# The low half of the gated rows by an accumulating DMA from GpSimd instead of a VectorE subtraction

## The chip, the cores and the metric

The kernel runs as one program on one core of one Trainium2 chip. The metric is the device time of one execution in microseconds (us), as the median of several executions; lower is better. The kernel before has a median of 2209.8 us over three runs (2206.93 to 2212.24). TensorE (PE) does the matrix products, VectorE (DVE) and ScalarE (ACT) the elementwise work, GpSimd (POOL) small copies and sums, and SyncE (SP) issues most of the loads and stores.

## The reference, cut to what matters

The program is one layer of a streaming encoder for 2048 prompt tokens and 64 sample tokens, with a model width of 1024. The first half (normalisation, input projection, pooling mixer, mLSTM memory, output projection) is not touched. The second half is a gated MLP with a causal convolution of width 3 between its two projections:

```
h2   = rmsnorm(x, g2) * (1 + sc2) + sh2
up   = h2 @ w_up                                   # 1024 -> 2 * 2816
conv = b_conv + sum(w_conv[j] * upp[:, j:j + T] for j in range(3))
a, g = jnp.split(conv, 2, -1)
x    = x + gt2 * ((jax.nn.silu(g) * a) @ w_down)   # 2816 -> 1024
```

All inputs and outputs are float32. The product silu(g) * a, channel by channel, is what this text calls the gated rows. They are the moving operand of the product with w_down.

## The kernel before, in words

**Halves.** TensorE takes operands that are rounded to a shorter float32 form (fp32r). So every operand X of a large product is kept as a high half (X rounded to that form, made by a copy on ScalarE) and a low half (X minus the high half, made by a subtraction on VectorE). A product is three passes: high by high, high weight by low row, low weight by high row. They stand in this order in the tuple PASSES.

**Tiling.** Tokens are handled transposed: channels on the 128 partitions, tokens along the row. The 2112 tokens of the MLP are three groups of 704, and a group is two halves of 352, the width of one matmul. The last group holds the end of the prompt and the 64 sample tokens, with separate pieces for each, so that an operation there is often two or three instructions. The 2816 inner channels are 22 tiles f of 128. Each group goes through them in four parts (PARTS) of 5, 5, 6 and 6 tiles. There are thus twelve parts in all, and 66 pairs (group, f), where a pair is one tile of a and the matching tile of g.

**The up phase of a part.** For each f, an object Pair makes a and g by seven products of 12 matmuls each (`Pair.products`, line 1522 records the matmuls), which share work between the two token halves by sums of weights and of rows. Between the products it issues steps of the pair before (old) and of the one before that (older). The steps of one pair, in their order, are:

- copy_u4, sum_g1, sum_a, sum_g0: the last sums out of the banks into the extended rows ea and eg (VectorE, line 1530). GpSimd first fills the two columns ahead of the row (line 1488).
- scale_a, scale_g: ta and tg, the convolution's first term, by ScalarE (line 1505). GpSimd then saves the row's last two columns (lines 1499 to 1502).
- taps_a, taps_g: the other two terms, two VectorE instructions each (line 1510).
- silu: on tg in place, ScalarE (line 1616).
- gate: tg = ta * tg, VectorE (line 1620).
- split_hi: the high half of the gated row, a ScalarE copy from tg to av (line 1637).
- split_lo: the low half, a VectorE subtraction of the high half from tg into the other half of av (line 1645).

The tile tg comes from a pool with one buffer (`t = f1.tile([P, EX], F32, tag="t" + tag, ...)`, the pool f1 having bufs=1). So scale_g of the next pair writes the bytes that split_hi and split_lo of this pair read. The tile av has six buffers, one for each pair of a part.

**The down phase of a part.** `down(ps, W, ks, secs)` multiplies the part's av tiles by tiles of w_down (line 1785): six matmuls of 352 columns for each k, three passes by two token halves. After each k it issues one of the steps that wait in the list `todo`. The order for a part with nf tiles is: n = 0 over k = 0 to nf-3; the remaining steps; the twelve matmuls of the last pair's last product; n = 1 over k = 0 to nf-3; k = nf-2 for n = 0 and 1; n = 2 over k = 0 to nf-2; k = nf-1 for n = 0, 1, 2; then the rows n = 3 to 7 in full. The next-to-last pair's split stands in `todo` under n = 0, and the last pair's steps from sum_g0 to split_lo stand under n = 1 and after. So av of the last two pairs is made while TensorE is already multiplying the earlier ones.

**What sets the order.** In this stage TensorE, ScalarE, VectorE and GpSimd run in the order of the program text (tc.manual_schedule). Each engine works its own list from the front and waits, at an instruction, for what that needs. SyncE's loads of weights run ahead of use through `pump`, which also issues the weights' own split into halves (ScalarE line 366, VectorE line 369). GpSimd has no DMA of its own before: every transfer is issued from SyncE or ScalarE.

Of the kernel before, what the change touches and what calls it, by code (L numbers as in the profile page):

```python
# [9 lines left out]
F32 = mybir.dt.float32  # L10
F32R = mybir.dt.float32r
AF = mybir.ActivationFunctionType
ALU = mybir.AluOpType
# [46 lines left out]
def tile_layer(ctx: ExitStack, tc: tile.TileContext, xT, vecs, cst, rst, rowv, w_mod, w_ada, w_qkou, w_v, w_pool,  # L60
               w_out, w_up, w_down, st_C, st_pool, yT, o_pool, o_C, o_m, o_conv):
    nc = tc.nc
    act, dve, pool, pe = nc.scalar, nc.vector, nc.gpsimd, nc.tensor
# [16 lines left out]
    def mm_ps():  # L80
        return bank("mm")
# [18 lines left out]
    def tick(i=0):  # L100
        q = bg[i]
        while q:
            try:
                next(q[0])
                return
            except StopIteration:
                q.pop(0)
# [54 lines left out]
    def pair_of(t, row, n):  # L162

        return t[:, :2 * row].rearrange("p (a t) -> p a t", a=2)[:, :, :n]
# [1310 lines left out]
    todo = []  # L1475

    def do(n=1):

        for _ in range(n):
            if todo:  # L1480
                todo.pop(0)()

    def both_of(a, b):
        return lambda: (a(), b())

    def ext_tile(o, f, tag):
        ext = f1.tile([P, EX], F32, tag="e" + tag, name="e" + tag, bufs=EB)
        pool.tensor_copy(ext[:, 0:2], UC[:, f, :])
        if o.last:
            pool.tensor_copy(ext[:, PT + 2:PT + 4], V[:, V_SC + 2 * f:V_SC + 2 * f + 2])  # L1490
        return ext
# [21 lines left out]
    def spans(o, half):  # L1513

        return [(pa, pb, a + 2 + 2 * s) for (i, pa, pb, a, b, s) in o.pieces if i == half]

    def product(ps, Bo, nm, first):
        pump()
        U = get_unit()
        for kc in range(4):  # L1520
            for pi, (a, b) in enumerate(PASSES):
                pe.matmul(ps[:, :FH], U[:, a, kc * P:(kc + 1) * P], Bo.at(nm, kc, b),  # L1522
                          start=(first and kc == 0 and pi == 0), stop=(kc == 3 and pi == 2), skip_group_check=not first)
            if kc % 2:
                tick(0)
        live[0] -= 1
# [5 lines left out]
    def half_tile(nm):  # L1532
        return f1.tile([P, FH], F32, tag=nm, name=nm)

    class Pair:
# [9 lines left out]
        def products(self, old):  # L1545


            o, Bo, f = self.o, self.Bo, self.f
            self.before = old
            older = old and old.before  # L1550
            b1, b2 = self.b1, self.b4 = mm_ps(), mm_ps()

            def rest(*steps):
                for pair, step in steps:
                    if pair:
                        step(pair)
            rest((old, Pair.copy_u4), (older, Pair.gate))
            product(b1, Bo, "B11", True)
            rest((old, Pair.sum_g1), (old, Pair.sum_a))
            self.s1 = half_tile("s1")  # L1560
            act.activation(self.s1, b1[:, :FH], AF.Copy)
            rest((older, Pair.split_hi))
            product(b2, Bo, "B21", True)
            rest((old, Pair.scale_a), (older, Pair.split_lo))
            if old:
                old.last_product()
            rest((old, Pair.taps_a), (old, Pair.sum_g0))
            product(b1, Bo, "T2", False)
            self.u2 = half_tile("u2")
            act.activation(self.u2, b1[:, :FH], AF.Copy)  # L1570
            rest((old, Pair.scale_g))
            self.ea = ext_tile(o, f, "a")
            for (a, b, d) in spans(o, 0):
                dve.tensor_tensor(out=self.ea[:, d:d + b - a], in0=b2[:, a:b], in1=self.s1[:, a:b], op=ALU.add)  # L1574
            self.b3 = mm_ps()
            product(self.b3, Bo, "T3", True)
            rest((old, Pair.taps_g))
            tick(1)
            product(self.b4, Bo, "B22", True)
            rest((old, Pair.silu))  # L1580
            product(b1, Bo, "T1", False)
# [40 lines left out]
        def split_hi(self):  # L1622
            t = f2.tile([P, XT], F32R, tag="av", name="av", bufs=6)
            self.apart = not (self.o.last and self.f >= PARTS[-1][0])
            if self.apart:
                d = t.rearrange("p (a h t) -> p a h t", a=2, h=2)
                w = NUDGE if self.i == 1 else 0
                self.cuts = [(lambda b, i=i, pa=pa, pb=pb: d[:, b, i, pa + w * b * i:pb + w * b * i], a + 2 * s, b + 2 * s)
                             for (i, pa, pb, a, b, s) in self.o.pieces] if self.o.last or w else [
                    (lambda b: d[:, b, :, :FH], 0, FT)]  # L1630
                self.av[self.i] = lambda b, lo, hi: d[:, b, lo // FH, w * b * (lo // FH):w * b * (lo // FH) + hi - lo]
            else:
                d = pair_of(t, 2 * XR, FT)
                self.cuts = [(lambda b, lo=a, hi=e: d[:, b, lo:hi], a + 2 * s, e + 2 * s) for (a, e, s) in self.o.segs]
                self.av[self.i] = lambda b, lo, hi: d[:, b, lo:hi]
            for cut, a, b in self.cuts:
                act.activation(cut(0), self.of_tg(cut(0), a, b), AF.Copy)  # L1637

        def of_tg(self, like, a, b):
            v = self.tg[:, a:b]  # L1640
            return v.rearrange("p (h t) -> p h t", h=2) if len(like.shape) == 3 else v

        def split_lo(self):
            for cut, a, b in self.cuts:
                dve.tensor_tensor(out=cut(1), in0=self.of_tg(cut(0), a, b), in1=cut(0).bitcast(F32), op=ALU.subtract)  # L1645

    def reload(Bo):
        for nm in BN:
# [104 lines left out]
    for o in fgroups:  # L1753
        Bo = B[o.g]
        for pi, (f0, f1_) in enumerate(PARTS):
# [4 lines left out]
            pair = None  # L1760
            for f in range(f0, f1_):
                old, pair = pair, Pair(o, Bo, f, f - f0, av)
# [17 lines left out]
            def down(ps, W, ks, secs, stays=False):  # L1780
                for k in ks:
                    U = W.at(k // 4)
                    for (a, b) in PASSES:
                        for i, (lo, hi) in enumerate(secs):
                            pe.matmul(ps[i][:, :hi - lo], U[:, a, k % 4 * P:(k % 4 + 1) * P], av[k](b, lo, hi),  # L1785
                                      start=(k == 0 and (a, b) == PASSES[0]), stop=(k == nf - 1 and (a, b) == PASSES[-1]))
                    if (k % 4 == 3 or k == nf - 1) and not stays:
                        live[0] -= 1
                    pump()
                    if todo:  # L1790
                        do()
                    else:
                        tick(1 - k % 2)
# [23 lines left out]

            old = pair.before
            pair.copy_u4()
            todo.extend([both_of(pair.sum_g1, old.gate), both_of(pair.sum_a, old.split_hi), both_of(old.split_lo, pair.scale_a)])  # L1820
            for n in range(NE - 1):
                pss.append([mm_ps() for _ in both])
                down(pss[n], Ws[n], range(nf - 2), both)
                if n == 0:
                    do(9)
                    pair.last_product()
                    todo.extend([both_of(pair.sum_g0, pair.scale_g), pair.taps_a, pair.taps_g, pair.silu, pair.gate,
                                 pair.split_hi, pair.split_lo])
            for n in range(NE - 1):
                down(pss[n], Ws[n], [nf - 2], both)  # L1830
            pss.append([mm_ps() for _ in both])
# [102 lines left out]
```

## Time and profile before

| what | value |
|---|---|
| median of three runs | 2209.8 us (2206.93 to 2212.24) |
| span of the profiled execution, first to last instruction | 2205.6 us |
| the median beyond that span | 4.2 us |
| TensorE busy | 2186.1 us, 99% of the span |
| VectorE busy | 1568.5 us, 71% |
| ScalarE busy | 1005.3 us, 46% |
| GpSimd busy | 203.0 us, 9% |
| mean granted clock of TensorE | 0.999 |
| line 1645, the subtraction | 112 instructions, 62.0 us |
| line 1637, the high half | 112 instructions, 56.2 us |

The profiled execution's own time is given by its span alone; the runs' times hold some us of start and end beside it. The gated rows are made from 828 to 2157 us of the span. The subtraction is 36 instructions of 704 columns, 32 of 352, 16 of 288 and 22 of 64, and 6 of 640 that are left. A row of a group reads: line, engine, operation, out<-in, shapes, count | busy us, mean ns of one | idle time of the engine just before them and what ended it. A row of the timeline reads: start in us, duration, engine, line, operation, count, and in brackets the engine's idle time before it and its releaser. Adjacent like instructions are merged into one row.

### The profile page before, as it was taken

Reading aid. Unit: us, or ns where it says so; the run is one execution under the profiler, and the core shown is the slowest. Engines: PE = TensorE matmul, PEld = TensorE weight load, DVE = VectorE, ACT = ScalarE, POOL = GpSimd, SP = SyncE. Lnnn points to the kernel's source line nnn. Section 1 sums busy time; section 2 is a strip of 40 time slices with the busy share of each in tenths; the row PEclk is TensorE's granted clock in tenths of the full one; section 3 lists DMA queues with packets and bytes.
Section 4 is the critical chain, followed back from the end, with each engine's and each line's share of the span. In section 5 each row is a group of like instructions: output and inputs, shape, how many; then the busy total and the mean of one; then the engine's idle time right before and its main releaser. Section 6 shows DMA issues by size and latency. Waiting matters only on the chain. (4 is left out here: it accounts for less than half of the span.)

```text
span 2205.6 us, 38165 instructions
## 1 busy us (share of the span) xinstructions
PE 2186.1 (99%) x13804; PEld 2079.2 (94%) x13804; DVE 1568.5 (71%) x2916; ACT 1005.3 (46%) x1993; POOL 203.0 (9%) x481
## 2 busy tenths in 40 slices
PE   8999999999999999999999999999999999999998
PEld 7888888888899999999999999999999999999998
DVE  5887669577765778787958587767667685767474
ACT  4653334235243455554636354545344443445354
POOL 0010000001000100010000210000001210101012
PEclk9999999999999999999999999999999999999999
DMA  9977987997898695767557876565458565353442
GB/s 355 367 242 264 333 275 243 324 324 239 292 323 272 223 310 177 234 205 239 188 173 233 266 245 200 183 214 175 144 169 285 186 190 166 111 173 121 150 148 81
DMA packets 279357, 498.58 MB, mean 226 GB/s; under 512 B 25176, under 2 KB 105432, under 8 KB 279168
## 3 DMA queue, kind: packets, MB, share of 16 engines
q1 hardware_dynamic: 267392, 468.05, 65.0%
q10 hardware_dynamic: 11776, 28.09, 3.4%
q8 instruction: 109, 1.79, 0.3%
q14 instruction: 80, 0.66, 0.1%
HBM read 385.29 MB, written 110.75 MB: 225 GB/s over the span
## 5 line engine op out<-in xcount | busy, mean ns | idle before, releaser
L1522 PE MATMUL mm<-hx,wt 128*128 128x352 f32 x5544 | 885.4, 321 | 1.0 <-DVE ea L1574 0.9
L1522 PEld LDWEIGHTS mm<-hx,wt 128*128 128x128 f32 x5544 | 879.5, 188 | 2.1 <-ACT wt L366 1.5
L1785 PE MATMUL mm<-av,wt 128*128 128x352 f32 (+2 forms) x3168 | 508.6, 321 | 0.4 <-DVE av L1645 0.3
L1785 PEld LDWEIGHTS mm<-av,wt 128*128 128x128 f32 x3168 | 502.6, 188 | 3.0 <-DVE av L1645 0.9
L423 PE MATMUL mm<-hl,wt 128*128 128x512 f32 (+2 forms) x1920 | 395.8, 358 | 1.7 <-DMA wt<-hl_kept 1.7
L366 ACT ACTIVATE wt<-raw 128x512 fp32r<-128x512 f32 (+3 forms) x494 | 274.5, 571 | 249.6 <-PE mm L1785 109.3
L369 DVE TENSOR_TENSOR wt<-raw,wt 128x512 fp32r<-128x512 f32 (+3 forms) x494 | 307.0, 637 | 87.5 <-ACT wt L366 81.4
L423 PEld LDWEIGHTS mm<-hl,wt 128*128 128x128 f32 x1920 | 312.6, 188 | 49.4 <-issue 5.3
L1800 DVE SCALAR_TENSOR_TENSOR x<-mm,MOD,x 128x352 f32<-128x352 f32 (+4 forms) x224 | 106.5, 526 | 128.8 <-PE mm L1785 128.8
L423 PE MATMUL mm<-mx,wt 128*128 128x512 f32 (+1 forms) x960 | 186.8, 353 | 0.0
L423 PEld LDWEIGHTS mm<-mx,wt 128*128 128x128 f32 x960 | 158.8, 188 | 25.4 <-ACT mx L1378 1.1
L1510 DVE SCALAR_TENSOR_TENSOR tg<-eg,V,tg 128x704 f32<-128x704 f32 (+1 forms) x132 | 125.7, 952 | 49.3 <-ACT tg L1505 46.8
L369 DVE TENSOR_TENSOR wt<-wt 128x512 fp32r<-128x512 f32 x176 | 121.8, 692 | 49.4 <-ACT wt L366 49.2
L366 ACT ACTIVATE wt<-wt 128x512 fp32r<-128x512 f32 x176 | 110.2, 626 | 75.1 <-DMA wt<-wsum 62.5
L1510 DVE SCALAR_TENSOR_TENSOR ta<-ea,V,ta 128x704 f32<-128x704 f32 (+1 forms) x132 | 125.6, 952 | 7.8 <-ACT ta L1505 5.4
L1645 DVE TENSOR_TENSOR av<-tg,av 128x704 fp32r<-128x704 f32 (+4 forms) x112 | 62.0, 588 | 43.2 <-ACT av L1637 43.0
L1570 ACT ACTIVATE u<-mm 128x352 f32<-128x352 f32 x66 | 30.6, 464 | 120.3 <-PE mm L1522 81.8
L1616 ACT ACTIVATE tg<-tg 128x704 f32<-128x704 f32 (+1 forms) x66 | 52.3, 793 | 68.9 <-DVE tg L1510 68.9
L203 DVE SCALAR_TENSOR_TENSOR acc<-raw,CA,acc 128x512 f32<-128x512 f32 x84 | 60.5, 744 | 32.1 <-DMA raw<-w_ada 32.1
L1530 DVE TENSOR_TENSOR eg<-mm,u 128x352 f32<-128x352 f32 x154 | 70.1, 467 | 18.4 <-ACT u L1585 11.2
L1114 PE MATMUL mm<-wt,hl 128*128 128x256 f32 (+1 forms) x576 | 70.9, 282 | 0.0
L1114 PEld LDWEIGHTS mm<-wt,hl 128*128 128x128 f32 x576 | 69.3, 188 | 1.0 <-issue 0.6
(299 smaller groups left out, 1951.9 us busy)
## 6 DMA issues: line engine op xcount, KB each, us to landing
wt<-hl_kept SPq DMA_DIRECT2D x108, 512.0 KB, 5.9
raw<-w_up SPq DMA_DIRECT2D x198, 256.0 KB, 3.1
wt<-wsum SPq DMA_DIRECT2D x176, 256.0 KB, 4.0
wt<-wsplit SPq DMA_DIRECT2D x88, 512.0 KB, 3.9
raw<-w_down SPq DMA_DIRECT2D x96, 256.0 KB, 3.9
w<-w_up SPq DMA_DIRECT2D x88, 256.0 KB, 5.4
wsum<-w SPq DMA_DIRECT2D x44, 512.0 KB, 5.7
wsplit<-wt SPq DMA_DIRECT2D x44, 512.0 KB, 5.0
```

The source lines that it names most:

```text
L203: dve.scalar_tensor_tensor(out=acc[s], in0=w, scalar=CA[:, k, s:s + 1], in1=acc[s], op0=ALU.mult, op1=ALU.add)
L366: act.activation(u.w[:, 0, :u.n], u.raw[:, :u.n], AF.Copy)
L369: dve.tensor_tensor(out=u.w[:, 1, :u.n], in0=u.raw[:, :u.n], in1=u.w[:, 0, :u.n].bitcast(F32), op=ALU.subtract)
L423: pe.matmul(ps[bi][:, :hi - lo], U[:, a, k % 4 * P:(k % 4 + 1) * P], mv[k][:, b, lo:hi], start=(at == 0 and pi == 0), stop=(k == order[-1] ...
L1114: pe.matmul(ps[ti][:n, :cols], h[4 * kh + k4][:, b, lo:lo + n], U[:, a, k4 % 2 * cols:(k4 % 2 + 1) * cols], start=(kh == 0 and k4 == 0 and ...
L1510: dve.scalar_tensor_tensor(out=t[:, :E], in0=ext[:, j:j + E], scalar=wc(j, f), in1=t[:, :E], op0=ALU.mult, op1=ALU.add)
L1522: pe.matmul(ps[:, :FH], U[:, a, kc * P:(kc + 1) * P], Bo.at(nm, kc, b), start=(first and kc == 0 and pi == 0), stop=(kc == 3 and pi == 2), ...
L1530: dve.tensor_tensor(out=ext[:, d:d + b - a], in0=ps[:, a:b], in1=u[:, a:b], op=ALU.add)
L1616: act.activation(self.tg[:, :E], self.tg[:, :E], AF.Silu)
L1645: dve.tensor_tensor(out=cut(1), in0=self.of_tg(cut(0), a, b), in1=cut(0).bitcast(F32), op=ALU.subtract)
L1785: pe.matmul(ps[i][:, :hi - lo], U[:, a, k % 4 * P:(k % 4 + 1) * P], av[k](b, lo, hi), start=(k == 0 and (a, b) == PASSES[0]), stop=(k == n ...
L1800: dve.scalar_tensor_tensor(out=x3[n][:, a:b], in0=ps[i][:, a - lo:b - lo], scalar=gt2(n, s), in1=x3[n][:, a:b], op0=ALU.mult, op1=ALU.add)
```

## The change

The step split_lo and its three calls go. Its work is put into split_hi. After the copies that make the high half, for each piece ScalarE writes the negated high half into the place of the low half, and GpSimd issues a DMA that adds the gated row from tg onto it. The source and the destination are both on chip. A 704-column piece carries 352 KB.

```diff
@@ Pair.products
-            rest((old, Pair.scale_a), (older, Pair.split_lo))
+            rest((old, Pair.scale_a))
@@ Pair.split_hi
             for cut, a, b in self.cuts:
                 act.activation(cut(0), self.of_tg(cut(0), a, b), AF.Copy)
+            for cut, a, b in self.cuts:
+                act.activation(cut(1), cut(0).bitcast(F32), AF.Copy, scale=-1.0)
+                pool.dma_start(out=cut(1).bitcast(F32), in_=self.of_tg(cut(0), a, b), accum_op=ALU.add)
...
-        def split_lo(self):
-            for cut, a, b in self.cuts:
-                dve.tensor_tensor(out=cut(1), in0=self.of_tg(cut(0), a, b), in1=cut(0).bitcast(F32), op=ALU.subtract)
@@ the down phase of a part
-            todo.extend([both_of(pair.sum_g1, old.gate), both_of(pair.sum_a, old.split_hi), both_of(old.split_lo, pair.scale_a)])
+            todo.extend([both_of(pair.sum_g1, old.gate), both_of(pair.sum_a, old.split_hi), pair.scale_a])
...
                     todo.extend([both_of(pair.sum_g0, pair.scale_g), pair.taps_a, pair.taps_g, pair.silu, pair.gate,
-                                 pair.split_hi, pair.split_lo])
+                                 pair.split_hi])
```

## The prediction

> **What bounds the kernel now.** I read the page first (span and busy time), then who waited for whom, then the groups by shape, and last the timeline around the ends of the parts, where the gated rows are needed soonest.
>
> ```profile
> span 2205.6 us, 38165 instructions
> ...
> PE 2186.1 (99%) x13804; PEld 2079.2 (94%) x13804; DVE 1568.5 (71%) x2916; ACT 1005.3 (46%) x1993; POOL 203.0 (9%) x481
> ```
>
> TensorE is busy in all but 19.5 us of the span (2205.6 - 2186.1), so work taken off VectorE gains only where TensorE waits for VectorE. The waits of TensorE from 829 to 2190 us, which cover every gated row, are two:
>
> ```profile
> PE mm L1522 <- DVE ea L1574: 0.9, 1, 0.9
> PE mm L1785 <- DVE av L1645: 0.3, 1, 0.3
> ```
>
> The most that the relief of VectorE can give is thus 1.2 us. The question is what the new path costs.
>
> **The change, part by part.** Removed and added, by groups, and the shape of 704 columns alone:
>
> ```profile
> L1645 DVE TENSOR_TENSOR av<-tg,av 128x704 fp32r<-128x704 f32 (+4 forms) x112 | 62.0, 588 | 43.2 <-ACT av L1637 43.0
> L1637 ACT ACTIVATE av<-tg 128x704 fp32r<-128x704 f32 (+4 forms) x112 | 56.2, 542 | 19.1 <-DVE tg L1620 18.3
> ```
> ```profile
> L1645 DVE TENSOR_TENSOR av<-tg,av 128x704 fp32r<-128x704 f32 x36 | 32.1, 891 | 24.0 <-ACT av L1637 24.0
> ...
> L1637 ACT ACTIVATE av<-tg 128x704 fp32r<-128x704 f32 x36 | 28.4, 788 | 11.2 <-DVE tg L1620 10.7
> ```
>
> VectorE loses 112 subtractions, 62.0 us. ScalarE gets 112 negations; each has the shape of the copy on line 1637, so I price them at the same 56.2 us, 0.79 us for 704 columns. ScalarE is busy 46% of the span, which covers this except where a gated row is awaited. GpSimd gets 112 DMAs. So 0.89 us on VectorE becomes 0.79 us on ScalarE plus X, the time from the end of the negation to the landing of the DMA.
>
> **X** has no row: nothing here goes from chip memory to chip memory, accumulates, or is issued by GpSimd. The nearest:
>
> ```profile
> hx<-Bd SPq DMA_DIRECT2D x61, 352.0 KB, 6.1
> Bd<-fscr ACTq DMA_DIRECT2D x56, 352.0 KB, 3.1
> ...
> raw<-w_down SPq DMA_DIRECT2D x48, 64.0 KB, 1.9
> ```
> ```profile
> L1748 POOL TENSOR_TENSOR ssum<-ssum,fscr 128x704 f32<-128x704 f32 x16 | 28.5, 1781 | 88.3 <-ACT fscr L1747 88.1
> ...
> L1488 POOL COPY eg<-UC 128x2 f32<-128x2 f32 x66 | 28.0, 424 | 250.1 <-DVE tg L1510 250.1
> ```
>
> The lower end is one plain trip of 352 KB, 3.1 us. The upper end is one trip out and one back, 3.1 + 6.1 = 9.2 us. Between them: 288 KB more cost 1.2 us (3.1 - 1.9), so 352 KB stream in 1.5 us beside a fixed 1.6 us. An accumulation reads both the row and its destination, so I count the stream twice, 1.6 + 3.0. For GpSimd's own issue I add its small copy, 0.42 us (the bounds are none, and its longest instruction, 1.78 us). **X = 5.0 us.**
>
> [...]
>
> **Where X falls on the path.** The second part of the second group has five tiles. The timeline at its end (matmuls, then the two last pairs' steps):
>
> ```profile
> 1439.18 2.06 PE L1522 MATMUL mm<-hx,wt 128*128 128x352 f32 x12
> 1439.49 0.79 ACT L1637 ACTIVATE av<-tg 128x704 fp32r<-128x704 f32 x1 [1.80 <-DVE tg L1620]
> 1440.31 0.89 DVE L1645 TENSOR_TENSOR av<-tg,av 128x704 fp32r<-128x704 f32 x1 [0.42 <-ACT av L1637]
> 1441.08 10.46 PE L1785 MATMUL mm<-av,wt 128*128 128x352 f32 x65
> 1442.20 0.98 ACT L1505 ACTIVATE tg<-eg,V 128x704 f32<-128x704 f32 x1 [0.56 <-DVE eg L1530]
> 1443.87 1.93 DVE L1510 SCALAR_TENSOR_TENSOR tg<-eg,V,tg 128x704 f32<-128x704 f32 x2
> 1445.84 0.79 ACT L1616 ACTIVATE tg<-tg 128x704 f32<-128x704 f32 x1 [2.65 <-DVE tg L1510]
> 1446.66 0.89 DVE L1620 TENSOR_TENSOR tg<-ta,tg 128x704 f32<-128x704 f32 x1 [0.86 <-ACT tg L1616]
> 1447.59 0.79 ACT L1637 ACTIVATE av<-tg 128x704 fp32r<-128x704 f32 x1 [0.44 <-DVE tg L1620]
> 1448.41 0.89 DVE L1645 TENSOR_TENSOR av<-tg,av 128x704 fp32r<-128x704 f32 x1 [0.66 <-ACT av L1637]
> ```
>
> Twelve matmuls take 1.90 us (1439.18 to 1441.08), 0.158 each. From 1441.08 TensorE does 18 + 12 + 24 matmuls and two of the first pass before it reads the last pair's low half: 56 x 0.158 = 8.85, at 1449.93. That half is ready at 1449.30 today, 0.6 us ahead. Every us added to this chain beyond 0.6 stops TensorE.
>
> X enters twice. First, the DMA of the next-to-last pair reads tg, and the one buffer of tg is written again by the last pair's scale_g. The copy ends at 1440.28, the negation at 1441.07, the DMA lands at 1446.07. scale_g starts then and not at 1442.20, and ends at 1447.05. The taps start there and not at 1443.87: 3.2 us late, and silu, gate and the copy behind them as much. Second, the last copy then ends at 1448.38 + 3.2, the negation 0.79 later, and the DMA lands at 1457.35. **Stall 7.4 us** (1457.35 - 1449.93); in general 2X - 2.6. The first pair's own low half (wanted at 1441.08 + 20 x 0.158 = 1444.24, landing at 1446.07) stops TensorE earlier, but inside the same 7.4 us.
>
> A part of six tiles, same steps:
>
> ```profile
> 1557.24 0.79 ACT L1637 ACTIVATE av<-tg 128x704 fp32r<-128x704 f32 x1 [0.85 <-DVE tg L1620]
> ...
> 1560.27 9.51 PE L1785 MATMUL mm<-av,wt 128*128 128x352 f32 x59
> 1561.09 0.98 ACT L1505 ACTIVATE tg<-eg,V 128x704 f32<-128x704 f32 x1 [1.36 <-DVE eg L1530]
> 1562.75 1.93 DVE L1510 SCALAR_TENSOR_TENSOR tg<-eg,V,tg 128x704 f32<-128x704 f32 x2
> ...
> 1566.47 0.79 ACT L1637 ACTIVATE av<-tg 128x704 fp32r<-128x704 f32 x1
> ```
>
> The first DMA runs from 1558.82 to 1563.82. scale_g ends at 1564.80, the taps are 2.05 late, the last negation ends at 1566.47 + 2.05 + 1.58 = 1570.10, and its DMA lands at 1575.10. TensorE wants it after 24 + 12 + 30 + 2 = 68 matmuls, at 1571.01. **Stall 4.1 us**; 2X - 5.9 for X above 3.
>
> The last group has three pieces for each row:
>
> ```profile
> 2020.66 0.98 ACT L1637 ACTIVATE av<-tg 128x352 fp32r<-128x352 f32 x3 [1.49 <-DVE tg L1620]
> ```
>
> That is 0.2 us more for the negations (0.98 - 0.79) and two more issues on GpSimd, 2 x 0.42: 1.0 us, twice in the chain, for four part ends: 8 us.
>
> **In the middle of a part** 42 of the 66 pairs (all but the last two of each part) have more time:
>
> ```profile
> 1425.47 0.79 ACT L1637 ACTIVATE av<-tg 128x704 fp32r<-128x704 f32 x1
> ...
> 1431.22 0.96 ACT L1505 ACTIVATE tg<-eg,V 128x704 f32<-128x704 f32 x1
> ...
> 1434.19 0.80 ACT L1616 ACTIVATE tg<-tg 128x704 f32<-128x704 f32 x1 [0.57 <-DVE tg L1510]
> ...
> 1436.51 0.47 ACT L1585 ACTIVATE u<-mm 128x352 f32<-128x352 f32 x1 [1.01 <-PE mm L1522]
> ```
>
> The DMA runs from 1427.05 to 1432.05, 0.8 us past the start of scale_g. ScalarE waits there, with the weights' halves (line 366) and silu queued behind it. Silu ends at 1435.8, still before ScalarE's copy at 1436.51, which waits for TensorE anyway. So I price it at nothing; the cover is gone at X = 5.7, and past it each us costs between nothing and 42 us. GpSimd's copies (lines 1488, 1502) queue behind the DMA for the 0.79 us of the negation and the issue. They come some 4 us apart and VectorE asks for them later, so this is nothing too. SyncE's queue is not passed by any step.
>
> **Sum.** 6 x 7.4 + 6 x 4.1 + 8 = 77 us, less at most 1.2. The profiled execution would have a span of 2205.6 + 76 = 2281.6. The median lies 4.2 us above this span (2209.8), so I forecast **2286 us**.
>
> **The rivals.**
>
> *The clock falls after each stall.* TensorE has no such gaps today, and its granted clock reads 1.00 at a part end and in the first 4 us, where it has nothing to do (busy columns PE, PEld, DVE, ACT, POOL, then the clock):
>
> ```profile
> 1436.30:1450.60 14.30, 14.30 (x93) 14.30 (x92) 11.16 (x19) 7.46 (x15) 1.24 (x4) 1.00 0.30 86
> ```
> ```profile
> 0.00:4.00 4.00, 0.00 (x0) 0.00 (x0) 0.48 (x1) 1.49 (x2) 2.78 (x21) 1.00 0.49 138
> ```
>
> If half the clock is granted for as long as the stall was, a mean stall of 5.8 us costs 2.9 more, twelve times 35: 2321 us. [...]
>
> *GpSimd is slow to issue because VectorE is busy.* Its copies do stretch beside line 1510:
>
> ```profile
> 1440.02 0.19 POOL L1502 COPY UC<-ea 128x2 f32<-128x2 f32 x1 [5.39 <-DVE ea L1530]
> ...
> 1444.11 0.75 POOL L1488 COPY ea<-UC 128x2 f32<-128x2 f32 x1 [3.78 <-DVE ta L1510]
> ```
>
> Four times as long, 0.75 against 0.19, and against it: only 0.56 us. If the issue suffered so throughout, X reaches its upper end, 9.2: 6 x 15.8 + 6 x 12.5 + 8 = 178 us, and half of 42 x 3.5 in the middles: 2461 us. It decides from X = 5.7.
>
> *One pass.* The accumulation reads its destination beside the source at no cost: X = 3.5, stalls 4.4 and 1.1, 41 us in all: 2251 us.
>
> *Not slower.* The DMA lands so soon that no row is late, and TensorE loses its waits for VectorE: 2209.8 - 1.2 = 2208.6 us. This needs X below 0.8 (1449.93 - 1449.17). Against it: 64 KB alone take 1.9.
>
> **How the numbers follow.** Forecast 50% (X from 4 to 6.5: 53 us, and 113 plus 17 of the middles: 2263 to 2340), clock 17%, slow issue 13%, one pass 15%, not slower 5%. The range leaves out most of slow issue and of not slower: from X = 3.1 (31 us, 2241) to X = 7 (125 and 27: 2362), with some us for rounding, 2237 to 2368. A difference within 0.2%, 4.4 us, can't be told from none; slower 0.95, the same 0.03, faster 0.02.
>
> **What would show it.** Line 1645 is gone. TensorE waits on line 1785 for a DMA into av, twelve times, longer at parts of five tiles than at six. ScalarE's line 1505 for tg waits for that DMA. The DMA's median to landing is X. I am wrong if the stalls lie in the middles, if X lies outside 3.1 to 9.2, or if the clock after a stall is under 1.

## The result, and the profile after

The changed kernel has a median of 2427.1 us over four runs (2421.2 to 2437.4), against 2210.2 for the kernel before: a ratio of 1.0988, 95% interval 1.0969 to 1.1007. It is slower by 217 us. The forecast was 2286 us with a range up to 2368. The sign was right, and the size was nearly three times the 76 us forecast.

The page of the changed kernel's profile, its span, busy times and the new group on GpSimd:

```profile
span 2435.2 us, 38498 instructions
...
PE 2264.9 (93%) x13804; PEld 2133.2 (88%) x13804; DVE 1517.7 (62%) x2804; ACT 1058.7 (43%) x2105; POOL 325.4 (13%) x593
...
L1640 POOL DMA_DIRECT2D av<-tg x112 | 111.2, 1146 | 394.9 <-ACT av L1639 304.3
L1505 ACT ACTIVATE tg<-eg,V 128x704 f32<-128x704 f32 (+1 forms) x66 | 64.3, 975 | 168.8 <-DMA av<-tg 168.7
```

The profiled execution took 2437.4 us; its span is 229.6 us longer than before (2435.2 - 2205.6). TensorE runs the same 13,804 matmuls, yet is busy 78.8 us longer (2264.9 - 2186.1) and idle 150.8 us longer (170.3 against 19.5). So two things grew: the waits, and the time of the matmuls themselves. VectorE lost 51 us of work, and nothing came of it. ScalarE waits 168.7 us at scale_g (line 1505) for the DMA. The waits of TensorE in the same profile:

```profile
PE mm L1784 <- DMA av<-tg: 89.2, 26, 8.9
PE mm L1522 <- DVE wt L369: 40.5, 29, 2.5
PE mm L1522 <- ACT wt L366: 6.8, 7, 2.3
PE mm L1784 <- DVE wt L369: 5.3, 5, 1.4
...
PE mm L1784 <- ACT wt L366: 4.3, 2, 2.3
```

The first row is the stall at the part ends, 89 us. Added up from the timeline part by part, 67 us of it lie at the eight part ends of the first two groups and 22 us at the four of the last group. The other four rows shown are new in kind: TensorE waits for halves of weights (lines 366 and 369), 57 us in all, and most of these waits are on line 1522, between products in the middle of parts. The landings in the DMA view, counted from the start of the issue, so that GpSimd's issue is in them:

```profile
av<-tg POOLq DMA_DIRECT2D x36, 352.0 KB, 6.5
...
av<-tg POOLq DMA_DIRECT2D x22, 32.0 KB, 5.3
```

An eleventh of the bytes (32 KB against 352) saves only 1.2 of 6.5 us. This hints that most of the time does not scale with size; the small pieces stand in the last group, behind larger ones, so it is no more than a hint. The end of the five-tile part of which the prediction was worked out, in the timeline (rows of the steps in the chain):

```profile
1549.52 0.79 ACT L1639 ACTIVATE av<-av 128x704 fp32r<-128x704 f32 x1
...
1550.74 1.22 POOL L1640 DMA_DIRECT2D av<-tg  x1 [6.84 <-PE mm L1522]
1556.24 6.26 PE L1784 MATMUL mm<-av,wt 128*128 128x352 f32 x36 [2.63 <-DMA av<-tg]
1556.28 0.98 ACT L1505 ACTIVATE tg<-eg,V 128x704 f32<-128x704 f32 x1 [4.70 <-DMA av<-tg]
...
1561.89 0.79 ACT L1639 ACTIVATE av<-av 128x704 fp32r<-128x704 f32 x1
...
1563.10 1.21 POOL L1640 DMA_DIRECT2D av<-tg  x1 [10.08 <-ACT fscr L741]
1571.36 2.13 PE L1784 MATMUL mm<-av,wt 128*128 128x352 f32 x6 [8.85 <-DMA av<-tg]
```

Both links of the chain are there. The first DMA holds TensorE and, through tg, scale_g at the same instant (1556.24 and 1556.28, 5.9 us after the negation ended at 1550.31). The second holds TensorE until 1571.36, 8.7 us after its negation (1562.68). Both stalls together are 11.5 us (2.63 + 8.85) where 7.4 was forecast. And a pair in the middle of a part:

```profile
862.21 0.79 ACT L1639 ACTIVATE av<-av 128x704 fp32r<-128x704 f32 x1
...
863.36 1.20 POOL L1640 DMA_DIRECT2D av<-tg  x1 [4.23 <-ACT av L1639]
...
869.90 0.98 ACT L1505 ACTIVATE tg<-eg,V 128x704 f32<-128x704 f32 x1 [2.09 <-DMA av<-tg]
870.78 1.14 ACT L366 ACTIVATE wt<-raw 128x512 fp32r<-128x512 f32 x2
870.91 1.94 DVE L1510 SCALAR_TENSOR_TENSOR tg<-eg,V,tg 128x704 f32<-128x704 f32 x2 [2.42 <-ACT tg L1505]
...
872.76 1.28 DVE L369 TENSOR_TENSOR wt<-raw,wt 128x512 fp32r<-128x512 f32 x2
...
873.50 2.49 PE L1784 MATMUL mm<-av,wt 128*128 128x352 f32 x14 [0.47 <-DVE wt L369]
```

X is 6.9 us here (863.00 to 869.90). ScalarE stands at scale_g; two halves of weights queued behind it start only at 870.78. VectorE's list has the taps of the same late row first (870.91 to 872.85), so its part of the weights starts at 872.76, and TensorE waits for that.

Last the granted clock, in stretches of 1 us of the changed kernel (columns: PE busy, PEld, DVE, ACT, POOL, then the clock), after a stall that began at 890.93:

```profile
892.00:893.00 1.00, 0.00 (x0) 0.00 (x0) 0.00 (x0) 0.00 (x0) 1.00 (x3) 1.00 0.41 156
893.00:894.00 1.00, 0.00 (x0) 0.00 (x0) 0.00 (x0) 0.00 (x0) 0.05 (x1) 0.65 0.79 124
894.00:895.00 1.00, 0.00 (x0) 0.00 (x0) 0.00 (x0) 0.00 (x0) 0.00 (x0) 0.50 1.14 176
896.00:897.00 1.00, 1.00 (x4) 1.00 (x5) 0.00 (x0) 0.00 (x0) 0.00 (x0) 0.50 0.00 0
899.00:900.00 1.00, 1.00 (x5) 1.00 (x5) 1.00 (x3) 0.62 (x1) 0.00 (x0) 0.50 0.29 82
900.00:901.00 1.00, 1.00 (x7) 1.00 (x6) 1.00 (x3) 0.46 (x2) 0.00 (x0) 0.94 0.00 0
...
902.00:903.00 1.00, 1.00 (x8) 1.00 (x8) 1.00 (x4) 1.00 (x2) 0.00 (x0) 1.00 0.83 209
```

The clock is halved while TensorE stands, 2.4 us into the stall, and stays so for some 4 us after it starts again at 895.92: four or five matmuls fall into a microsecond instead of eight. Over the kernel the granted clock is 0.969 on the mean, against 0.999. The sum over all the halved stretches of the changed kernel:

```profile
sum 151.64, PE 109.64 PEld 108.09 DVE 76.18 ACT 47.71 POOL 9.17; mean PE 4.22 PEld 4.16 DVE 2.93 ACT 1.83 POOL 0.35
```

TensorE is busy in 109.64 us of them, and at half the clock that costs 55 of the 78.8 us by which it is busy longer. The other 24 us go with the number of waits, 92 against 16 before: matmuls overlap in a stream (0.158 us each, where one on line 1522 lasts 0.326 on the mean of the page), and the last ones before a wait run out alone. Two matmuls between two waits, shown in the last section, take 0.59 us and not 0.32. That this makes all of the 24 us is an argument from these counts and was not tested by itself.

### The profile page after: what moved, and what is told of

Read it like the earlier page. It is cut to its first block, busy times and chain, and to the rows that moved or that the text cites. A ratio compares the mean times of both kernels' runs of the same rounds, so it can differ in the third digit from the quotient of the medians.

```text
span 2435.2 us, 38498 instructions
## 1 busy us (share of the span) xinstructions
PE 2264.9 (93%) x13804; PEld 2133.2 (88%) x13804; DVE 1517.7 (62%) x2804; ACT 1058.7 (43%) x2105; POOL 325.4 (13%) x593
## 3 DMA queue, kind: packets, MB, share of 16 engines
q1 hardware_dynamic: 267392, 468.05, 58.5%
## 5 line engine op out<-in xcount | busy, mean ns | idle before, releaser
L1522 PE MATMUL mm<-hx,wt 128*128 128x352 f32 x5544 | 914.9, 326 | 51.3 <-DVE wt L369 40.5
L1522 PEld LDWEIGHTS mm<-hx,wt 128*128 128x128 f32 x5544 | 895.8, 190 | 66.1 <-DVE wt L369 49.1
L1784 PE MATMUL mm<-av,wt 128*128 128x352 f32 (+2 forms) x3168 | 555.6, 337 | 99.0 <-DMA av<-tg 89.2
L1784 PEld LDWEIGHTS mm<-av,wt 128*128 128x128 f32 x3168 | 539.2, 200 | 112.4 <-DMA av<-tg 97.2
L1640 POOL DMA_DIRECT2D av<-tg x112 | 111.2, 1146 | 394.9 <-ACT av L1639 304.3
L1505 ACT ACTIVATE tg<-eg,V 128x704 f32<-128x704 f32 (+1 forms) x66 | 64.3, 975 | 168.8 <-DMA av<-tg 168.7
L1502 POOL COPY UC<-ea 128x2 f32<-128x2 f32 x44 | 46.3, 1053 | 299.2 <-DVE ea L1530 299.2
L1488 POOL COPY eg<-UC 128x2 f32<-128x2 f32 x66 | 33.6, 510 | 332.8 <-DVE tg L1510 332.8
```

Of the source, the lines that this page charges most:

```text
L1505: act.activation(t[:, :E], ext[:, 2:2 + E], AF.Identity, scale=wc(2, f), bias=V[:, V_BC + f:V_BC + f + 1])
L1640: pool.dma_start(out=cut(1).bitcast(F32), in_=self.of_tg(cut(0), a, b), accum_op=ALU.add)
```

## The experiments

The theory after this reading had three parts: stalls at the part ends, stalls in the middles through the hold of tg, and a lower clock after both. All ratios are to the kernel before.

| kernel | median us | ratio (95% interval) |
|---|---|---|
| the change | 2427.1 | 1.0988 (1.0969 to 1.1007) |
| DMA in the middles only | 2299.2 | 1.0407 (1.0391 to 1.0422) |
| DMA at the ends only | 2337.6 | 1.0581 (1.0563 to 1.0598) |
| the change, two buffers for tg | 2305.8 | 1.0432 (1.0416 to 1.0448) |
| negation, VectorE adds | 2217.3 | 1.004 (1.0025 to 1.0055) |
| plain copy from GpSimd | 2321.9 | 1.051 (1.0479 to 1.054) |
| plain copy from ScalarE | 2345.0 | 1.0614 (1.0584 to 1.0645) |
| accumulation of 8 columns | 2321.0 | 1.0506 (1.0465 to 1.0547) |
| the change, 624 unused matmuls | 2424.7 | 1.0975 (1.0943 to 1.1007) |
| the change, 360 unused matmuls | 2412.6 | 1.0925 (1.091 to 1.094) |
| middles only, two buffers for tg | 2224.9 | 1.0075 (1.0062 to 1.0089) |
| before, u4 in the buffer of s1 | 2213.3 | 1.002 (1.0011 to 1.0029) |

### Middles and ends apart

Two kernels, each with the DMA for some pairs and VectorE's subtraction, at its old places, for the others:

```diff
+            self.by_dma = not self.f >= next(e for s, e in PARTS if s <= self.f < e) - 2
+            for cut, a, b in self.cuts if self.by_dma else ():
+                act.activation(cut(1), cut(0).bitcast(F32), AF.Copy, scale=-1.0)
+                pool.dma_start(out=cut(1).bitcast(F32), in_=self.of_tg(cut(0), a, b), accum_op=ALU.add)
...
         def split_lo(self):
-            for cut, a, b in self.cuts:
+            for cut, a, b in () if self.by_dma else self.cuts:
```

The second kernel has the same without the "not".

> The accumulating DMA only for the 42 pairs in the middle of a part; the last two pairs of each part keep VectorE's subtraction. Theory: the one buffer of tg holds ScalarE at scale_g until the DMA has landed, and the weights' halves queued behind it come late, so the waits of TensorE on line 1522 (some 50 us in the changed kernel, 40.5 of them for VectorE's line 369) stay, with some 10 to 25 us of lower clock: 2265 to 2290 us. Rival, the middles suffer only from what the part ends leave behind: 2210 us.

> The accumulating DMA only for the last two pairs of each part; the middle pairs keep VectorE's subtraction. Theory: the waits of TensorE for the DMA into av (89.2 us in the changed kernel) stay, and the clock falls after them, some 25 to 60 us: 2325 to 2360 us, and the gains over before of this kernel and of the one with only the middles add up to the whole 217 us. Rival, all is in the ends: 2427 us.

Measured: the middles cost 89.7 us (2299.2 - 2209.5), the ends 128.0 us (2337.6 - 2209.5). Their sum, 217.7, is the whole loss of 217. So neither is a tail of the other, and the middles, 9 us above their range, are 41% of it. In the kernel with the middles only, TensorE's waits are again mainly those for weights, and none is for the DMA:

```profile
PE mm L1522 <- DVE wt L369: 39.5, 27, 2.4
PE mm L1789 <- DVE wt L369: 4.6, 5, 1.6
PE mm L1522 <- ACT wt L366: 4.5, 6, 1.7
```

In the kernel with the ends only there is one wait of size:

```profile
PE mm L1789 <- DMA av<-tg: 84.8, 25, 9.2
```

TensorE is busy 34 us longer than before in the first (2220.1) and 44 us in the second (2230.1). Together that is the 78.8 us of the change. By the halved stretches, as above, the clock is 16 of the 34 us (TensorE busy in 32.64 us of them, 65 waits) and 41 of the 44 us (81.18 us, 40 waits). So the lower clock is mostly a matter of the ends, and in the middles about half of the longer busy time comes with the waits themselves.

### The hold of tg

```diff
-        t = f1.tile([P, EX], F32, tag="t" + tag, name="t" + tag)
+        t = f1.tile([P, EX], F32, tag="t" + tag, name="t" + tag, bufs=2 if tag == "g" else 1)
...
-            self.u4 = half_tile("u4")
+            self.u4 = half_tile("s1")
```

> The changed kernel with two buffers for tg (room made by letting the half tile u4 share the buffer of s1). Nothing holds scale_g any more. Theory: the middles cost nothing, X enters the chain at a part's end once and not twice. With X at 6.9 us the last low half is 6.9 - 0.8 = 6.1 us late at parts of five tiles, and 2 us less or 4 late at parts of six: some 61 us, 8 more in the last group, and 20 to 30 of clock: 2290 to 2310 us. Rival, the hold of tg plays no part and the DMA's own lateness is all: 2427 us.

Measured 2305.8 us: 121 us of the loss are gone with a second buffer. Its waits are 51.8 us for the DMA at the ends, where X now enters once, and none for line 369 in the middles. The time is in the expected range, with less waiting at the ends than the 69 us expected:

```profile
PE mm L1784 <- DMA av<-tg: 51.8, 23, 5.9
```

With the same second buffer and the DMA in the middles alone:

> The accumulating DMA for the 42 middle pairs only, and two buffers for tg (u4 shares the buffer of s1): no chain at a part's end holds a DMA and nothing holds scale_g. Theory: the 90 us of the middles came from the hold alone and are gone; VectorE's relief gives at most 1 us: 2207 to 2214 us. Rival, the negations on ScalarE, GpSimd's issues or the DMA traffic cost in the middles too: 2225 us or more.

Measured 2224.9 us, at the rival's edge. The hold of tg was 74 of the 90 us of the middles (2299.2 - 2224.9). Sixteen stay, and their waits are for line 1574, 10.4 us in 11 waits, with TensorE busy 6.7 us longer than before (2192.8):

```profile
PE mm L1522 <- DVE ea L1574: 10.4, 11, 2.5
```

So the side edit was run alone, on the kernel before:

> The kernel before with one edit: the half tile u4 shares the buffer of s1, as in the two kernels with two buffers for tg. Control for that side edit: the 16 us that the middles with two buffers cost over before, and their 10 us of waits for line 1574. If the sharing makes them: 2220 to 2225 us. If the negation, GpSimd's issues or the DMA make them: 2207 to 2213 us.

Measured 2213.3 us, 4.4 us over before, with 4.3 us of waits for line 1574. The shared buffer is thus some 4 of the 16 us, and the hold of tg some 79 of the 90, if the two add up. The other 12 come with the negation, the issue or the transfer in the middles, and these runs do not divide them. No version with the DMA is as fast as the kernel before.

### The negation alone

```diff
+            for cut, a, b in self.cuts:
+                act.activation(cut(1), cut(0).bitcast(F32), AF.Copy, scale=-1.0)
...
-                dve.tensor_tensor(out=cut(1), in0=self.of_tg(cut(0), a, b), in1=cut(0).bitcast(F32), op=ALU.subtract)
+                dve.tensor_tensor(out=cut(1), in0=self.of_tg(cut(0), a, b), in1=cut(1).bitcast(F32), op=ALU.add)
```

> No DMA: ScalarE negates the high half as in the change, and VectorE adds tg onto it, at the places of its former subtraction. Prices the 112 negations alone. Theory: 0.8 us on the chain at the part ends, of which 0.6 is covered at parts of five tiles and all at parts of six: 2210 to 2214 us. Rival, ScalarE's added 56 us are a cause of their own: 2230 us or more.

Measured 2217.3 us, 7.7 over before and above the range of the theory. TensorE waits at the ends for VectorE's half, six times 0.8 us:

```profile
PE mm L1787 <- DVE av L1647: 4.8, 6, 1.0
```

The six waits are at the six parts of five tiles in the three groups. The theory counted the negation once in the chain, 0.8 us less a margin of 0.6. It is there twice, as the end of the same part as in the prediction shows:

```profile
1443.91 9.04 PE L1787 MATMUL mm<-av,wt 128*128 128x352 f32 x56
1443.97 0.90 DVE L1647 TENSOR_TENSOR av<-tg,av 128x704 fp32r<-128x704 f32 x1 [1.25 <-ACT av L1639]
...
1451.24 0.79 ACT L1637 ACTIVATE av<-tg 128x704 fp32r<-128x704 f32 x1 [0.43 <-DVE tg L1620]
```

VectorE's addition for the next-to-last pair waits for the negation and starts 0.06 us after the matmuls; before, the subtraction started 0.77 us ahead of them (1440.31 and 1441.08). The taps behind it in VectorE's list are late by this, so that the last pair's copy starts 7.33 us after the matmuls instead of 6.51. Then comes the last pair's own negation. Twice 0.8 less 0.6 is 1.0, and the wait there is 0.89 us. The 56 us on ScalarE are still no cause of size.

### What X is made of

```diff
-                pool.dma_start(out=cut(1).bitcast(F32), in_=self.of_tg(cut(0), a, b), accum_op=ALU.add)
+                pool.dma_start(out=cut(1).bitcast(F32), in_=self.of_tg(cut(0), a, b))
```

> The changed kernel with a plain copy in place of the accumulation, still issued by GpSimd: the low half then holds the whole gated row, and the subtraction is left out. Theory A, the accumulation reads twice and costs a second stream: X falls by some 1.5 us, 12 ends x 2 x 1.5 less, some 36 to 60 us less than 2427: 2365 to 2390 us. Theory B, the fixed path from GpSimd is the price: within 10 us of 2427.

Measured 2321.9 us: 105 us come back, more than either theory said. The plain copy of 352 KB lands after 5.4 us instead of 6.5; its issue, which is part of that, takes 0.61 us instead of 1.15. With 0.4 us ahead of the issue X is then some 5.8 us, close to the edge of 5.7 that the prediction named for the middles, and the waits for line 369 on line 1522 fall from 40.5 to 11.9 us. In the same kernel with act.dma_start:

> The same plain copy, issued by ScalarE directly behind its negation (the subtraction is left out again). Theory B, the path from GpSimd is the price: its issue of 1.2 us falls to ScalarE's 0.33 and the landing to the 3.2 us of ScalarE's other transfers of 352 KB, X about 3.5: 2240 to 2270 us. Theory A: as with the plain copy from GpSimd.

Measured 2345.0 us, slower than from GpSimd. The expectation failed in two ways. 352 KB still take 5.1 us to land, and a DMA in ScalarE's list waits there for the negation ahead of it. From that kernel's timeline:

```profile
863.69 0.79 ACT L1639 ACTIVATE av<-av 128x704 fp32r<-128x704 f32 x1
864.51 0.63 ACTq L1640 DMA_DIRECT2D av<-tg  x1
865.18 0.63 ACT L366 ACTIVATE wt<-wt 128x512 fp32r<-128x512 f32 x1 [0.70 <-ACT av L1639]
865.72 0.96 ACT L1505 ACTIVATE ta<-ea,V 128x704 f32<-128x704 f32 x1
```

The issue costs ScalarE 0.7 us ahead of ta; the taps and line 1574 behind them come late, and TensorE waits 35.6 us for line 1574, in 42 waits. The accumulation with few bytes:

```diff
-                pool.dma_start(out=cut(1).bitcast(F32), in_=self.of_tg(cut(0), a, b), accum_op=ALU.add)
+                lo, g = cut(1).bitcast(F32), self.of_tg(cut(0), a, b)
+                part = (slice(None),) * (len(lo.shape) - 1) + (slice(0, 8),)
+                pool.dma_start(out=lo[part], in_=g[part], accum_op=ALU.add)
```

> The changed kernel with each accumulation cut to 8 columns of each row piece; the rest of the low half stays the negated high half (the addition of the other columns is left out). Theory B, fixed cost: X falls only from some 6.9 to 5 us, time 2340 to 2390 us. Theory A, bytes: X falls to about 3 us, time 2225 to 2245 us.

Measured 2321.0 us, as with the plain copy, and 19 us under theory B's range. Four and eight KB land after 4.4 and 4.6 us:

```profile
av<-tg POOLq DMA_DIRECT2D x76, 4.0 KB, 4.4
av<-tg POOLq DMA_DIRECT2D x36, 8.0 KB, 4.6
```

So of 6.5 us some 4.4 need almost no bytes. That kernel keeps 111 us of the 217 us of loss. What the 4.4 us are was asked with nothing else issued, by four transfers of each of four kinds in a row behind the last store of the kernel before (accumulation, plain, accumulation of 8 columns, plain from ScalarE; the time of that kernel says nothing of the change):

```diff
+    for _ in range(4):
+        pool.dma_start(out=qa, in_=q0, accum_op=ALU.add)
+    for _ in range(4):
+        pool.dma_start(out=qp, in_=qa)
...
```

> The kernel before, and behind its last store four transfers of each of four kinds, each waiting for the one before it, with nothing else moving: accumulations of 352 KB from GpSimd, plain copies of it from GpSimd, accumulations of 8 columns from GpSimd, plain copies from ScalarE. Theory, much of X is the wait behind the loads' traffic: each lands some 2 us sooner than in the kernel, accumulation about 4 us, plain about 3, 8 columns about 2. Rival, X is the path's own cost: 6.5, 5.4 and 4.4 us as in the kernel.

```profile
qa<-q POOLq DMA_DIRECT2D x4, 352.0 KB, 3.8
...
qp<-qa POOLq DMA_DIRECT2D x4, 352.0 KB, 2.5
...
qb<-qp POOLq DMA_DIRECT2D x4, 4.0 KB, 2.0
```

Alone they land after 3.8, 2.5 and 2.0 us; in the kernel after 6.5, 5.4 and 4.4. (For the plain copies from ScalarE the profile gives no landing.) So for each of the three kinds some 2.4 to 2.9 us are added in the kernel, whatever its bytes. The kernel with 8 columns suggests where they come from, since its transfers bring almost no traffic of their own. Their landings, from the view of line 1642:

```profile
DMA to landing us min/median/max: 2.0/4.4/7.9
```

The fastest equals the one alone. Sorted by how busy the DMA engines were in the 3 us from the issue, the 16 transfers under 40% have a median of 2.5 us, and the 66 over 80% one of 5.3. What keeps them busy is mainly SyncE's queue with the loads (58.5% of the span on the changed kernel's page, against 6.3% for GpSimd's queue). The two go together; that the loads are the cause is not shown, since they were not varied by themselves. Adding cost 1.3 us over a plain copy alone (3.8 - 2.5), and an accumulation of 352 KB cost 1.8 us over one of almost no bytes (3.8 - 2.0).

### The clock

Unused matmuls in TensorE's list, before the two places where it waits at a part's end (spin(n) issues n of them into a bank that nobody reads):

```diff
+            spin(16)
             for n in range(NE - 1):
                 down(pss[n], Ws[n], [nf - 2], both)
...
+            spin(36)
             for n in range(NE):
                 down(pss[n], Ws[n], [nf - 1], both)
```

> The changed kernel with unused matmuls in TensorE's list ahead of the two places at a part's end where it waits for a low half: 16 (2.5 us) ahead of the first, 36 (5.7 us) ahead of the second; the result is never read. Theory: they fill the stalls, the clock no longer falls at the part ends, and 20 to 50 us come back although there is more work: 2375 to 2410 us. Rival, the lower clock is not due to the stalls: 2427 us or, where a stall is shorter than the filling, more.

Measured 2424.7 us, no difference from the change that its interval could show. By the time alone the rival would hold. The trace tells why it does not. The waits for the DMA fell from 89.2 to 14.1 us, but 624 matmuls of 0.158 us are 98.6 us, 24 more than the stalls they filled. TensorE's busy time without them is 2331.7 - 98.6 = 2233.1, 32 us less than in the change, and the clock is 0.987 instead of 0.969; by the halved stretches, TensorE loses 26 us to the clock instead of 55. So the gain was there and was spent. With fewer (for parts of five tiles 12 and 24, of six 0 and 28, in the last group 10 and 16):

> As the changed kernel with unused matmuls at the part ends, but fewer (some 360 of them, 57 us, against 624 and 99 us), so that the filling stays shorter than the stalls. Theory, the clock falls because TensorE stands still: waits fall by the 57 us that are filled, and some 20 us of lower clock come back: 2395 to 2412 us. Rival: 2427 us.

Measured 2412.6 us, 14 us faster than the change and clear of its interval, though 0.6 us past the slow edge of what was expected. It does 57 us of matmuls that nobody reads. Its view of waits and its page:

```profile
PE mm L1784 <- DMA av<-tg: 37.8, 22, 5.9
```
```profile
PE 2293.7 (95%) x14164; PEld 2165.0 (90%) x14164; DVE 1515.0 (63%) x2804; ACT 1058.8 (44%) x2105; POOL 326.9 (14%) x593
```

Without the 56.9 us of the 360 extra matmuls TensorE is busy 2236.8 us, 28 less than in the change. In both kernels the only edit gives TensorE work ahead of its stalls, and the clock rises from 0.969 to 0.987 and 0.985: in these runs the lower clock at the part ends is caused by TensorE's standing still.

## Why the prediction was right and wrong

**Where the sum failed.** The profiled execution is 229.6 us longer. TensorE waits 89 us of that for the DMA at the part ends, where the sum has 77. It waits 57 us for halves of weights, mostly in the middles, where the sum has nothing. It is busy 79 us longer, where the sum has nothing either. The step that failed is "So I price it at nothing", for the middles, together with the X of 5.0 us on which it rests. The second is the clock, which stood among the rivals and was left out of the sum. Two of the prediction's own signs of being wrong came: stalls in the middles, and a clock under 1 after a stall.

**What held.** TensorE gained nothing from VectorE's relief. The chain at the part ends has the two links that were worked out: the second buffer took one of them away and the waits there fell from 89 to 52 us. The sign followed from that.

**X (forecast 5.0, measured 6.9 in the middle, 5.9 and 8.7 at the end shown).** The term that was too small is "a fixed 1.6 us", read from a load of 64 KB on another queue. With the 0.42 us for GpSimd's issue it makes 2.0 us, which is what a transfer of almost no bytes takes alone, issue included. In the kernel that takes 4.4 us, of which the issue is 1.15 on the mean. The doubled stream was over-sized: 3.0 us, against 2.1 in the kernel (6.5 - 4.4) and 1.8 alone. Some 0.4 us between the negation and the issue were not in the sum. So 4.4 + 2.1 + 0.4 = 6.9 stands in place of 2.0 + 3.0 = 5.0.

**The part ends.** The forecast of 77 us came near the 89 measured because two errors pull apart. The eight part ends of the first two groups stall 67 us, where 46 was forecast (4 x 7.4 + 4 x 4.1): X was too low. The formulas themselves hold there. In the kernel with the ends only, 352 KB land after 5.8 us and start 0.4 us after the negation; with X = 6.2 the formulas give 4 x 9.8 + 4 x 6.5 = 65 us for these eight, and 65 were measured. The four part ends of the last group stall 22 us, where 31 was forecast (2 x 7.4 + 2 x 4.1 + 8). They were taken to be dearer for their three pieces and are cheaper: in the kernel with the ends only these pieces land after 3.0 to 4.2 us.

**The middles.** "I price it at nothing" was the costliest step: 90 us. Its text had the right place (ScalarE waits at scale_g, with the halves of weights behind it) and an edge, 5.7 us, which X passed. The slack beyond the edge was misjudged. The cover named was ScalarE's own copy; but the halves of weights come due sooner, and 57 us of TensorE's waits in the change are for them. By that text, 1.2 us past the edge at 42 pairs would have been at most 50 us. In the kernel with the middles only TensorE stands 59 us longer than before (78.6 against 19.5), and is busy 34 us longer, 16 of them by the clock.

**The clock.** It was the rival held at 17%, priced at 35 us, and it was not in the sum. It took 55 us in the change, and 41 in the kernel with the ends only, for which the 35 were meant. That the halving lasts as long as the stall was the author's estimate; after 2.4 us of the stall of 4.99 us that began at 890.93 the clock stood at 0.50 for 6.8 us, 4.2 of them with TensorE at work again. The row of the first 4 us, which reads 1.00 with TensorE idle, was a poor witness against it: the trace has no record of the clock before 8.1 us of the span, and a stretch without one reads 1.00. The same profile has a better witness at its end, where TensorE is idle too:

```profile
2205.00:2206.00 1.00, 0.00 (x0) 0.00 (x0) 0.00 (x0) 0.00 (x0) 0.00 (x0) 0.50 0.00 0
```

**The other rivals.** A slow issue on GpSimd was not the cause: 1.15 us is under the 1.78 us bound. But its time, 2461, built on X near its upper end with the middles paying, was nearest to the result of 2427, for the wrong reason: that nearness is luck. One pass and not slower fell with X. The range ended too low because the clock was left out of its upper case, and because the middles, with X = 7, were in it at 27 us where they cost 90.

## What to carry to other kernels

Before work is moved off an engine that is not the bound, ask what the replacement keeps waiting: here a DMA of 6 us took the place of an instruction of 0.9, and because it still read a tile with one buffer, the wait passed to an engine with other work queued. Count the fixed time of a transfer as it is in the traffic of the kernel (here 4.4 us, and 2.0 alone), not that of a small load on another queue. Where TensorE is busy 99% of the time, price each new wait with the clock that it will lose after it (here 55 us, beside 151 us of longer idling).

## What the runs showed that was not expected

**The clock fell after short gaps too.** In the middle of a part of the changed kernel:

```profile
2192.00:2193.00 1.00, 0.59 (x2) 0.30 (x2) 0.96 (x2) 0.48 (x1) 0.00 (x0) 1.00 0.00 0
2193.00:2194.00 1.00, 0.00 (x0) 0.00 (x0) 1.00 (x3) 0.55 (x1) 0.43 (x1) 0.89 0.00 0
2194.00:2195.00 1.00, 0.93 (x3) 0.93 (x4) 1.00 (x3) 1.00 (x3) 0.66 (x2) 0.50 0.00 0
...
2197.00:2198.00 1.00, 1.00 (x8) 1.00 (x7) 0.02 (x1) 0.62 (x2) 0.00 (x0) 0.91 0.68 207
```

Two gaps of 0.54 and 1.47 us, with two matmuls between them, are all the waits that the timeline shows from 2178.22 to 2194.07. The halved stretch runs from about 2193.8 (0.89 of that microsecond is 0.2 us at half) to 2197.2: 3.4 us. The stall at 890.93 gave 6.8 us, twice as long (893.3 to 900.1). The length of the last gap alone did not tell when the clock fell: it fell 2.4 us into that stall and here with no gap over 1.5 us, while a gap of 2.98 us that ended at 884.68 left it at 1.00. What made the difference no run shows.

**GpSimd's small copies behind an accumulating DMA were slower.** The copy on line 1502 out of ea takes 1.05 us on the mean in the changed kernel (46.3 us in 44), and 0.41 before (17.9 us in 44). With the plain copy from GpSimd it takes 0.25 (11.0 us in 44), so it is not any DMA of GpSimd's that slows it. VectorE waited for it once here, 0.7 us.
